# A convolution gate's projection moves from the attention's filler work to a Strassen section of the gate stage

## The chip, the cores and the metric

The kernel runs on one NeuronCore of a Trainium2 chip. The metric is the device time of one execution in microseconds (us), lower is better. TensorE (PE) does the matrix products, VectorE (DVE), ScalarE (ACT) and GpSimd (POOL) the elementwise work, and SyncE (SP), ACT and POOL issue transfers between the memory outside the core (HBM) and the on-chip memory SBUF. Products land in PSUM, which has eight banks of 128 x 512 float32.

## The reference

One layer of a hybrid block, 1024 tokens by 1024 channels, float32. Cut to what matters here:

```python
h = rmsnorm(x, ln1_g) * (1.0 + sc1) + sh1
p = h @ w_in
q, k, v, cb, cc, cx, ga, gb = split(p)          # eight sections of 1024 columns
q, k = rmsnorm(q per head), rmsnorm(k per head) # 16 heads of 64
y_a = stick_breaking_attention(q, k, v)         # strictly causal, 128-query blocks
y_b = cb * causal_dwconv(cc * cx, conv_w)       # conv over three tokens
merged = sigmoid(ga) * (y_a @ w_branch_a) + sigmoid(gb) * (y_b @ w_branch_b)
x = x + g1 * (merged @ w_out)
h = rmsnorm(x, ln2_g) * (1.0 + sc2) + sh2
x = x + g2 * ((silu(h @ w_ffn_gate) * (h @ w_ffn_up)) @ w_ffn_down)
```

In the attention, with z the scaled product of a query and a key, a weight is sigmoid(z) times the product of (1 - sigmoid(z)) over the keys between that key and the query. No softmax is needed, but a running product along the keys is.

## The kernel before, in words

Every float32 product is made of three PE matmuls: each operand is split into a rounded high part and the low rest, and high x high, high x low and low x high are summed in PSUM. The splits are made by one ACT copy and one DVE subtraction, and weights pass through them after they are loaded.

The stages, in order:

- **Start** (to about 205 us): norm statistics, v and k, the factors of h for the next stage, kept in HBM (`d_t`) or in the four large tiles `hh`, `hl`, one pair per half of the tokens.
- **Gate stage** (about 205 to 587 us): five sections of the input projection, in the list `gates`: q (section 5), conv C and conv x (1 and 2, by turns), the two branch gates (4 and 3). A section has four entries, each of two row blocks j and j+4 by two token halves. An entry uses a seven-product form of Strassen (in the Winograd variant): seven half products `half_prod` (lines 131 to 133) of 12 matmuls each in place of eight. POOL forms the sums of weights (`ws`), ACT and DVE split them, DVE combines the products (`c11`, `c12`, `c21`, `c22`), and `put` hands each of the four results on. `later` runs deferred work; for q that is `put_q`, two splits for each result.
- **Attention** (about 587 to 981 us): 16 heads of eight query blocks i, 128 steps s in all. A step computes the scores z of its block (lines 914 and 915), ACT takes the sigmoid (916), POOL masks the diagonal block (919), DVE runs the scan of products over every second key (929) and POOL fills in the other half (137). The transposes of a block (943) come LAG steps later, here two; ACT (946) and DVE (947) split what they give into `ath` and `atl`, and one step after the second block of a pair the product with v follows (958 and 959, tile `o`). So the order in which PE runs them is fixed: PE takes its instructions in the order in which they were written, and so do DVE and POOL for the attention's own.
- Between the attention's instructions stand **fillers**: groups of three matmuls (`mm_ch`, lines 1019 to 1021) of work that needs no attention result. A planner spreads them: each piece of attention work has a cost (`F_Z`, `F_T`, `F_S`), the sum is `ta`, and `fill` emits filler groups, counted as 0.65 each, up to `ta * ratio`. The first HEAD groups run ahead of the first scores, TAIL is kept for the end. The fillers are the conv B projection (section 0) times the convolution's result, 16 tiles of eight groups, and then the product of that with `w_branch_b`, again 16 tiles of eight groups.
- **Later stages**: the product with `w_branch_a`, the output projection, the FFN.

Of the conv branch: `put_u` writes the convolution's result to HBM (`d_y`); the filler loads it (`cy`), multiplies it by its product, splits that and writes it to `d_yb`; the second half of the fillers loads `d_yb` into the four large tiles. Since the gate stage overwrites part of `hh[1]`, `hl[1]` with a factor, that part is first saved to `d_h` and loaded again when the gate stage ends.

SP, ACT and POOL each run their transfers' issues in order. In the built program a transfer issued from SP or ACT also waits for the one eight earlier among those of both.

## Time and profile before

| | |
|---|---|
| times of three runs | 1794.98, 1796.44, 1798.49 us; median 1796.44 |
| profiled execution | 1797.03 us, span 1795.0 us |
| TensorE clock granted, mean | 0.999 |
| busy | PE 1781.7, DVE 1270.1, ACT 829.6, POOL 343.3 us |

A span is the time from the first to the last instruction; the device time holds 2.0 us more. A row "L1019 PE MATMUL pj<-big,whi ... x256 | 113.2, 442" reads: line 1019 of the kernel, engine PE, output tile `pj` from inputs `big` and `whi`, 256 of them, 113.2 us in all, 442 ns each. PE's matmuls are pipelined, so that the length of one says little; what counts is the distance between two starts. A wait in brackets, as in "[2.41 <-POOL pt L137]", is the idle time ahead of an instruction and what ended it.

### The profile page before, as it was taken

Reading aid. Unit: us, or ns where it says so; the run is one execution under the profiler, and the core shown is the slowest. Engines: PE = TensorE matmul, PEld = TensorE weight load, DVE = VectorE, ACT = ScalarE, POOL = GpSimd, SP = SyncE. Lnnn points to the kernel's source line nnn. Section 1 sums busy time; section 2 is a strip of 40 time slices with the busy share of each in tenths; the row PEclk is TensorE's granted clock in tenths of the full one; section 3 lists DMA queues with packets and bytes.
Section 4 is the critical chain, followed back from the end, with each engine's and each line's share of the span. In section 5 each row is a group of like instructions: output and inputs, shape, how many; then the busy total and the mean of one; then the engine's idle time right before and its main releaser. Section 6 shows DMA issues by size and latency. Waiting matters only on the chain.

```text
span 1795.0 us, 24911 instructions
## 1 busy us (share of the span) xinstructions
PE 1781.7 (99%) x8599; PEld 1485.0 (83%) x8599; DVE 1270.1 (71%) x2030; ACT 829.6 (46%) x1553; POOL 343.3 (19%) x437
## 2 busy tenths in 40 slices
PE   8999999999999999999999999999999999999999
PEld 6888877888888788888888888888888888888887
DVE  6876486687774677777776764698877787644776
ACT  5534364333433567776675221764544454432321
POOL 0023333823231244333332100100000000000000
PEclk9999999999999999999999999999999999999999
DMA  9579654222644977796655866334533444389876
GB/s 379 163 240 376 246 192 141 88 87 98 221 152 142 279 209 190 198 326 177 165 139 183 277 223 217 123 106 159 217 129 137 156 174 158 131 331 351 263 233 222
DMA packets 165009, 359.07 MB, mean 200 GB/s; under 512 B 15538, under 2 KB 60938, under 8 KB 163732
## 3 DMA queue, kind: packets, MB, share of 16 engines
q1 hardware_dynamic: 128300, 289.65, 49.3%
q10 hardware_dynamic: 33096, 55.25, 8.7%
q0 software_dynamic: 3488, 12.59, 2.1%
q8 instruction: 68, 1.11, 0.3%
q14 instruction: 57, 0.47, 0.1%
HBM read 247.84 MB, written 109.62 MB: 199 GB/s over the span
## 4 chain that ended last, share of the span: by engine, by line
PE 96%; DMA 2%; ACT 1%; DVE 0%; issue 0%; POOL 0%; SPq 0%; POOLq 0%; DVEq 0%; ACTq 0%
PE e L132 8%; PE e L133 8%; PE e L131 8%; PE pj L131 7%; PE pj L133 7%; PE pj L132 7%; PE pj L294 7%; PE pj L1019 5%; PE pj L1020 5%; PE pj L1021 5%; PE e L1613 4%; PE e L1614 4%; PE e L1615 4%; PE tr L943 3%; PE o L959 2%; PE z L914 2%
## 5 line engine op out<-in xcount | busy, mean ns | idle before, releaser
L1229 ACT ACTIVATE whi<-raw 128x512 fp32r<-128x512 f32 x137 | 84.9, 628 | 159.6 <-PE e L132 101.0
L1230 DVE TENSOR_TENSOR wlo<-raw,whi 128x512 fp32r<-128x512 f32 x137 | 93.1, 687 | 70.2 <-ACT whi L1229 52.8
L137 POOL TENSOR_TENSOR pt<-pt 128x63 f32<-128x63 f32 (+7 forms) x128 | 101.5, 793 | 212.8 <-DVE pt L929 196.5
L132 PE MATMUL e<-big,whi 128*128 128x512 f32 x352 | 136.9, 389 | 0.0
L131 PE MATMUL e<-big,whi 128*128 128x512 f32 x352 | 136.5, 390 | 0.0
L133 PE MATMUL e<-big,wlo 128*128 128x512 f32 x352 | 136.1, 389 | 0.0
L294 PE MATMUL pj<-whi,big 128*128 128x512 f32 x448 | 132.9, 393 | 2.7 <-ACT big L263 2.7
L947 DVE TENSOR_TENSOR atl<-tr,ath 128x512 fp32r<-128x512 f32 (+1 forms) x192 | 104.0, 553 | 34.0 <-ACT ath L946 32.7
L137 DVE TENSOR_TENSOR c<-pj,c 128x512 f32<-128x512 f32 x140 | 93.4, 683 | 47.6 <-PE pj L133 47.0
L131 PE MATMUL pj<-big,whi 128*128 128x512 f32 x320 | 125.0, 391 | 0.0
L133 PE MATMUL pj<-big,wlo 128*128 128x512 f32 x320 | 124.8, 390 | 0.0
L132 PE MATMUL pj<-big,whi 128*128 128x512 f32 x320 | 124.6, 389 | 0.0
L1614 PE MATMUL e<-wlo,f 128*128 128x512 f32 (+1 forms) x319 | 121.8, 382 | 0.0
L1613 PE MATMUL e<-whi,f 128*128 128x512 f32 (+1 forms) x319 | 121.6, 382 | 0.0
L1615 PE MATMUL e<-whi,f 128*128 128x512 f32 (+1 forms) x319 | 121.6, 382 | 0.0
L916 ACT ACTIVATE pt<-z,rq 128x128 f32<-128x128 f32 (+1 forms) x192 | 107.3, 579 | 25.7 <-PE z L915 23.0
L1019 PE MATMUL pj<-big,whi 128*128 128x512 f32 x256 | 113.2, 442 | 0.0
L137 DVE TENSOR_TENSOR wlo<-raw,whi 128x512 fp32r<-128x512 f32 x108 | 86.2, 802 | 30.6 <-ACT whi L517 30.4
L946 ACT ACTIVATE ath<-tr 128x512 fp32r<-128x512 f32 (+1 forms) x192 | 93.1, 488 | 28.6 <-PE tr L943 27.6
L131 PE MATMUL e<-rh,whi 128*128 128x512 f32 x264 | 102.7, 389 | 0.0
L132 PE MATMUL e<-rl,whi 128*128 128x512 f32 x264 | 102.7, 389 | 0.0
L294 PEld LDWEIGHTS pj<-whi,big 128*128 128x128 f32 x448 | 84.4, 189 | 21.8 <-ACT big L263 4.2
(301 smaller groups left out, 4736.9 us busy)
## 6 DMA issues: line engine op xcount, KB each, us to landing
f<-d_f SPq DMA_DIRECT2D x77, 512.0 KB, 4.5
d_f<-fs SPq DMA_DIRECT2D x70, 512.0 KB, 3.4
raw<-w_cg SPq DMA_DIRECT2D x40, 512.0 KB, 3.7
raw<-w_u SPq DMA_DIRECT2D x26, 512.0 KB, 4.2
raw<-w_g SPq DMA_DIRECT2D x25, 512.0 KB, 4.3
raw<-w_kv SPq DMA_DIRECT2D x20, 512.0 KB, 5.0
ld<-ada SPq DMA_DIRECT2D x16, 512.0 KB, 7.0
d_t<-ts SPq DMA_DIRECT2D x16, 512.0 KB, 6.7
```

The lines of the kernel that those rows point to most:

```text
L131: nc.tensor.matmul(ps, wh[:, k, :], fh[:, k, :], start=(k == 0 and not onto), stop=False, skip_group_check=onto)
L132: nc.tensor.matmul(ps, wh[:, k, :], fl[:, k, :], start=False, stop=False, skip_group_check=onto)
L133: last = nc.tensor.matmul(ps, wl[:, k, :], fh[:, k, :], start=False, stop=(k == 3), skip_group_check=onto)
L137: eng.tensor_tensor(out=out, in0=a, in1=b, op=op)
L294: nc.tensor.matmul(ps, a, b, start=(k == 0 and q == 0), stop=(k == KT - 1 and q == 2))
L916: nc.scalar.activation(pt[:, off + s0:off + s0 + m], z[:, :m], AF.Sigmoid, scale=rq[:, 1, i, h:h + 1])
L946: nc.scalar.activation(th[:, :nb, c0:c0 + P], src, AF.Copy)
L947: nc.vector.tensor_tensor(out=tl[:, :nb, c0:c0 + P], in0=src, in1=th[:, :nb, c0:c0 + P].bitcast(F32), op=ALU.subtract)
L1019: nc.tensor.matmul(ps, wh, rh_, start=(k == 0), stop=False)
L1613: nc.tensor.matmul(o, sh, w[0][:, c], start=(j == 0), stop=False)
L1614: nc.tensor.matmul(o, sh, w[1][:, c], start=False, stop=False)
L1615: nc.tensor.matmul(o, sl, w[0][:, c], start=False, stop=(j == NJ - 1))
```

## The change

Conv B is taken out of the fillers and becomes a further section (0) of the gate stage's list, behind conv C and x and ahead of the branch gates. `load_y` loads the convolution's result for an entry's two row blocks, and `put_b`, called from `later`, multiplies, splits and writes to `d_yb`, on the ACT queue. The save and reload of `d_h` go. The four large tiles are allocated in another order, so that the fillers' first pair, `yh[0]`, `yl[0]`, takes the place of `hh[0]`, `hl[0]`; the second pair is loaded later.

The attention's transposes come three steps behind the scores (LAG), the product with v four steps behind (DAV), with six tiles `pt` in place of five. The first head's q, k and v are loaded from the POOL queue, and the second head's loads no longer wait in the planned order for the first head's. HEAD falls from 16 to 4, the fillers' total is halved, and up to 5.0 units (EARLY) of it are moved to the attention's first steps.

```diff
-    hh = [big() for n in range(2)]
-    hl = [big() for n in range(2)]
+    hh, hl = [], []
+    for n in range(2):
+        hh.append(big())
+        hl.append(big())
...
-             [(sec, j) for sec in (4, 3) for j in range(4)])
+             [(sec, j) for sec in (0, 4, 3) for j in range(4)])
...
+    def load_y(m):
+        ys[m] = g_big()[:, :T]
+        nc.sync.dma_start(ys[m], d_y[m])
+
+    def put_b(c, m, n):
+
+        hl_ = gp.tile([P, 2, 512], F32R, tag=("sq", "tr")[n], bufs=2, name=nm("gt"))
+        tt(nc.vector, c, c, ys[m][:, n * 512:(n + 1) * 512], ALU.mult)
+        nc.scalar.activation(hl_[:, 0], c, AF.Copy)
+        tt(nc.vector, hl_[:, 1], c, hl_[:, 0].bitcast(F32), ALU.subtract)
+        for e in range(2):
+            nc.scalar.dma_start(d_yb[e][n][:, m, :], hl_[:, e].bitcast(F32))
...
+        if sec == 0:
+            load_y(j)
+            load_y(j + 4)
...
+            elif sec == 0:
+                pendb.append((c, m, n))
...
+            if pendb:
+                put_b(*pendb.pop(0))
...
-    NPT = 5
+    NPT, LAG = 6, 3
...
-    NZ, NTR, NPJ, DAV, KQ = 2, 3, 2, 3, 1
+    NZ, NTR, NPJ, DAV, KQ = 2, 3, 2, LAG + 1, 1
...
-                    with tc.issue_after(lastld[0].ins):
+                    with tc.issue_after(lastld[0].ins) if h else ExitStack():
                         att_load(h + 1)
...
-            tr_ = att_trans(*steps[s - 2]) if 0 <= s - 2 < len(steps) else iter(())
+            tr_ = att_trans(*steps[s - LAG]) if 0 <= s - LAG < len(steps) else iter(())
...
-        cb_w = {}
-        for m, n in [(m + d, n) for m in range(0, KT, 2) for n in range(2) for d in range(2)]:
...
-                mm_ch(ps, w, hh[n], hl[n], kk, kk + KQ)
-            nc.vector.tensor_tensor(out=y, in0=ps, in1=y, op=ALU.mult)
...
+        load_yb(0)
         wb = {}
...
+            if (m, n) == (1, 0):
+                with tc.issue_after(lastld[0].ins):
+                    load_yb(1)
...
-    FILL = 2.0 * 16 * 5.2
+    FILL = 16 * 5.2
-    HEAD, TAIL = 16, 10.0
+    HEAD, TAIL, EARLY = 4, 10.0, 5.0
-    ratio = (FILL - TAIL) / ATT
+    ratio = (FILL - TAIL - EARLY) / ATT
...
-        att_load(0)
+        att_load(0, nc.gpsimd)
+        vl = load_vlast(0, nc.gpsimd)
+        turn_vlast(0, vl)
+        load_v(0, 1, nc.gpsimd)
+        load_v(0, 0, nc.gpsimd)
...
-            fill(min(ta * ratio, FILL - TAIL) + 1.3 * nfl)
+            fill(min(ta * ratio + min(1.5 * ta, EARLY), FILL - TAIL) + 1.3 * nfl)
```

The rows that follow are the built programs' instruction order, engine by engine; line numbers are each kernel's own. PE's order around the first transposes, from the transposes of `vl` (v's last rows) on; `pj` is a filler, `z` the scores, `tr` transposes. Before:

```order
L871 MATMUL tr_5149<-dm,vl_5115 64x9 x8
L1019 MATMUL pj_5243<-big_144,whi_5130 128x512
L1020 MATMUL pj_5243<-big_146,whi_5130 128x512
L1021 MATMUL pj_5243<-big_144,wlo_5131 128x512
L914 MATMUL z_5250<-skh_5120,sqt_5119 128x256
L915 MATMUL z_5250<-skl_5121,sqt_5119 128x256
L914 MATMUL z_5262<-skh_5120,sqt_5119 128x384
L915 MATMUL z_5262<-skl_5121,sqt_5119 128x384
L1019 MATMUL pj_5243<-big_144,whi_5130 128x512
L1020 MATMUL pj_5243<-big_146,whi_5130 128x512
L1021 MATMUL pj_5243<-big_144,wlo_5131 128x512
L943 MATMUL tr_5272<-dm,pt_5110 128x128
```

After:

```order
L890 MATMUL tr_5808<-dm,vl_5793 64x9 x8
L933 MATMUL z_5890<-skh_5798,sqt_5797 128x384
L934 MATMUL z_5890<-skl_5799,sqt_5797 128x384
L1038 MATMUL pj_5846<-big_5826,whi_5838 128x512
L1039 MATMUL pj_5846<-big_5827,whi_5838 128x512
L1040 MATMUL pj_5846<-big_5826,wlo_5839 128x512
L933 MATMUL z_5915<-skh_5798,sqt_5797 128x512
L934 MATMUL z_5915<-skl_5799,sqt_5797 128x512
L1038 MATMUL pj_5942<-big_5826,whi_5924 128x512
L1039 MATMUL pj_5942<-big_5827,whi_5924 128x512
L1040 MATMUL pj_5942<-big_5826,wlo_5925 128x512
L962 MATMUL tr_5946<-dm,pt_5787 128x128
```

Ahead of these rows stand, before, only the first block's scores; after, those, two filler groups, the second block's scores and one more group. So five filler groups and three further blocks' scores now lie between the first scores and their transposes, where there were two groups and two blocks.

PE's order where the first head ends, from the second transposes of block 5 on, with the product with v of blocks 4 and 5 (`o`); in both kernels four transposes of block 5 and one filler group stand just ahead. Before:

```order
L943 MATMUL tr_5456<-dm,pt_5110 128x128 x2
L914 MATMUL z_5472<-skh_5279,sqt_5278 128x128
L915 MATMUL z_5472<-skl_5280,sqt_5278 128x128
L1019 MATMUL pj_5442<-big_144,whi_5196 128x512
L1020 MATMUL pj_5442<-big_146,whi_5196 128x512
L1021 MATMUL pj_5442<-big_144,wlo_5197 128x512
L943 MATMUL tr_5484<-dm,pt_5111 128x128 x4
L1019 MATMUL pj_5442<-big_144,whi_5196 128x512
L1020 MATMUL pj_5442<-big_146,whi_5196 128x512
L1021 MATMUL pj_5442<-big_144,wlo_5197 128x512
L958 MATMUL o_5494<-ath_5385,vt_5259 128x256
L959 MATMUL o_5494<-atl_5386,vt_5259 128x256
```

After:

```order
L962 MATMUL tr_6125<-dm,pt_5786 128x128 x2
L933 MATMUL z_6132<-skh_5906,sqt_5905 128x256
L934 MATMUL z_6132<-skl_5907,sqt_5905 128x256
L962 MATMUL tr_6141<-dm,pt_5787 128x128 x4
L977 MATMUL o_6148<-ath_6058,vt_5887 128x256
L978 MATMUL o_6148<-atl_6059,vt_5887 128x256
```

Both filler groups between the transposes and the product that uses them are gone here.

SP's order when the attention begins: the loads of the second filler pair and of the second head (`sqt`, `skh`, `skl`). Before, from the reload of `d_h` on:

```order
L1099 DMA big_146<-d_h_88 128x2048
L1099 DMA big_144<-d_h_87 128x2048
L834 DMA sqt_5119<-d_q_63 64x1024
L835 DMA skh_5120<-d_k_65 64x8x128
L836 DMA skl_5121<-d_k_66 64x8x128
```

After, the end of the second pair's eight loads and the start of the second head's:

```order
L1055 DMA big_5932<-d_yb_70 128x1024
L1056 DMA big_5933<-d_yb_72 128x1024
L505 DMA raw_7536<-w_b 128x1024
L1045 DMA sgi_5822<-d_sgb 128x512
L853 DMA sqt_5905<-d_q_63 64x1024
L854 DMA skh_5906<-d_k_65 64x8x128
L855 DMA skl_5907<-d_k_66 64x8x128
```

Before, SP loads 2 MB of `d_h` and then the first head; after, it loads 8 MB of `d_yb` in two pairs, the second of which waits for the gate stage's last product, and then the second head.

More of the change, by code (lines that the diff above doesn't have):

```diff
@@ L81, in block_kernel @@
     d_t = {q: drp.tile([P, 2, 4, 512], F32, name=f"d_t{q}") for q in (6, 3, 5, 4)}
-    d_h = [drp.tile([P, 4, 512], F32, name=f"d_h{e}") for e in range(2)]
     ident = const.tile([P, P], F32, name="dm")
@@ L833, in att_load, with load_v @@
             es = slice(e * DH, (e + 1) * DH)
-            nc.sync.dma_start(sqt[es].bitcast(F32), d_q[e][pr, e0:e0 + DH, :])
-            nc.sync.dma_start(skh[es].rearrange("p (i t) -> p i t", t=P).bitcast(F32), d_k[0][pr // 4][:, e0:e0 + DH, pr % 4].rearrange("i p t -> p i t"))
-            nc.sync.dma_start(skl[es].rearrange("p (i t) -> p i t", t=P).bitcast(F32), d_k[1][pr // 4][:, e0:e0 + DH, pr % 4].rearrange("i p t -> p i t"))
+            q.dma_start(sqt[es].bitcast(F32), d_q[e][pr, e0:e0 + DH, :])
+            q.dma_start(skh[es].rearrange("p (i t) -> p i t", t=P).bitcast(F32), d_k[0][pr // 4][:, e0:e0 + DH, pr % 4].rearrange("i p t -> p i t"))
+            q.dma_start(skl[es].rearrange("p (i t) -> p i t", t=P).bitcast(F32), d_k[1][pr // 4][:, e0:e0 + DH, pr % 4].rearrange("i p t -> p i t"))
         hd[h] = (sqt, skh, skl)
-    def load_v(h, e):
+    def load_v(h, e, q=nc.sync):
         pr = h // 2
@@ L844, in load_v @@
         vab[t_] = first_va if (h, e) == (0, 1) else v_tile(e)
-        lastld[0] = nc.sync.dma_start(vab[t_], d[e:P + e])
+        lastld[0] = q.dma_start(vab[t_], d[e:P + e])
     def att_dv(h, part):
@@ L1023, in fillers @@
     def fillers():
-        cb_w = {}
-        for m, n in [(m + d, n) for m in range(0, KT, 2) for n in range(2) for d in range(2)]:
-            if n == 0:
-                with tc.issue_after(lastld[0].ins) if m > 1 else ExitStack():
-                    cb_w[m] = load_ch(w_cg[0, m])
-            w = cb_w[m]
-            y = fp.tile([P, 512], F32, tag="st", bufs=3, name=nm("cy"))
-            nc.sync.dma_start(y, d_y[m, :, n * 512:(n + 1) * 512])
-            ps = ps_f()
-            for kk in range(0, KT, KQ):
-                if kk:
-                    yield 0.65 * KQ
-                mm_ch(ps, w, hh[n], hl[n], kk, kk + KQ)
-            nc.vector.tensor_tensor(out=y, in0=ps, in1=y, op=ALU.mult)
-            yh = fq.tile([P, 512], F32R, tag="ybh", bufs=2, name=nm("ybh"))
-            yl = fq.tile([P, 512], F32R, tag="ybl", bufs=2, name=nm("ybl"))
-            nc.scalar.activation(yh, y, AF.Copy)
-            nc.vector.tensor_tensor(out=yl, in0=y, in1=yh.bitcast(F32), op=ALU.subtract)
-            nc.sync.dma_start(d_yb[0][n][:, m, :], yh.bitcast(F32))
-            nc.sync.dma_start(d_yb[1][n][:, m, :], yl.bitcast(F32))
-            yield 0.65 * KQ
         def load_sb(m, n):
@@ L1051, in fillers, with load_yb @@
         yh, yl = [], []
-        for n in range(2):
+        def load_yb(n):
             yh.append(big())
```

20 lines of the change are left out of this document (5 added, 15 removed).

## The prediction

> **What bounds the kernel now.** I read the page first: busy times, slices, and the chain that ended last.
>
> ```profile
> span 1795.0 us, 24911 instructions
> PE 1781.7 (99%) x8599; PEld 1485.0 (83%) x8599; DVE 1270.1 (71%) x2030; ACT 829.6 (46%) x1553; POOL 343.3 (19%) x437
> PEclk9999999999999999999999999999999999999999
> PE 96%; DMA 2%; ACT 1%; DVE 0%; issue 0%; POOL 0%; SPq 0%; POOLq 0%; DVEq 0%; ACTq 0%
> ```
>
> PE is busy 99% of the span at the full clock and is 96% of the chain. So a change pays by PE time that it removes, less any wait that it opens on PE. The view by stretches shows which engines could open one:
>
> ```profile
> 205.00:281.00 76.00, 76.00 (x335) 59.90 (x334) 60.53 (x89) 45.76 (x79) 24.17 (x16) 1.00 0.56 196
> 434.00:587.00 153.00, 153.00 (x678) 126.63 (x677) 105.27 (x153) 58.68 (x98) 40.83 (x29) 1.00 0.50 170
> 587.00:598.00 11.00, 11.00 (x50) 9.13 (x49) 1.98 (x3) 2.37 (x4) 0.00 (x0) 1.00 0.86 259
> 598.00:981.00 383.00, 379.07 (x2340) 329.43 (x2339) 294.56 (x504) 264.12 (x588) 144.31 (x260) 1.00 0.74 206
> ```
>
> The columns are the length, then busy time of PE, PEld, DVE, ACT and POOL, clock, DMA share, GB/s. The rows are the q section, the branch-gate sections, the 16 filler groups ahead of the first scores, and the attention. PE has no idle time in the first three and 3.9 us in the attention, nearly all at its start.
>
> **The PE work.** Distances between starts on PE's timeline:
>
> ```profile
> 584.73 0.39 PE L131 MATMUL pj<-big,whi 128*128 128x512 f32 x1
> ...
> 587.45 0.39 PE L1019 MATMUL pj<-big,whi 128*128 128x512 f32 x1
> ...
> 598.33 0.22 PE L914 MATMUL z<-skh,sqt 128*128 128x128 f32 x1
> ...
> 707.48 0.60 PE L943 MATMUL tr<-dm,pt 128*128 128x128 f32 x4
> 707.84 0.48 PE L1019 MATMUL pj<-big,whi 128*128 128x512 f32 x1
> 708.15 0.40 PE L1020 MATMUL pj<-big,whi 128*128 128x512 f32 x1
> 708.39 0.39 PE L1021 MATMUL pj<-big,wlo 128*128 128x512 f32 x1
> 708.62 0.38 PE L943 MATMUL tr<-dm,pt 128*128 128x128 f32 x2
> 708.76 0.30 PE L914 MATMUL z<-skh,sqt 128*128 128x128 f32 x1
> 708.90 0.28 PE L915 MATMUL z<-skl,sqt 128*128 128x128 f32 x1
> 709.01 0.44 PE L1019 MATMUL pj<-big,whi 128*128 128x512 f32 x1
> ...
> 709.76 0.60 PE L943 MATMUL tr<-dm,pt 128*128 128x128 f32 x4
> 710.11 0.48 PE L1019 MATMUL pj<-big,whi 128*128 128x512 f32 x1
> ...
> 710.89 0.28 PE L958 MATMUL o<-ath,vt 128*128 128x256 f32 x1
> ```
>
> A half product of 12 takes 587.45 - 584.73 = 2.72 us, 0.2267 each. In the attention a filler matmul takes about 0.235 (708.15 to 708.39 to 708.62), and 0.31 (707.84 to 708.15) behind transposes.
>
> Removed: conv B as filler, 16 tiles x 8 x 3 = 384 matmuls. By the two instruction orders 336 of them leave the stretch between the first scores and the last product with v (705 fillers there become 369): 336 x 0.235 = 79.0 us. The extra 0.08 behind transposes does not leave with a filler, since something else then follows; but the places where another instruction follows transposes fall from 194 to 171, 23 x 0.08 = 1.8. The other 48 stood ahead of the scores (16 groups become 4) or behind the attention: 48 x 0.2267 = 10.9. Together -91.7 us.
>
> Added: four gate entries of 7 x 12 matmuls, 336 x 0.2267 = 76.2 us, if none waits. Its cover: `put_b` has per result two DVE operations, one ACT copy and two ACT issues, while `put_q` has two DVE operations, three ACT ones and two issues; and the q section above runs PE without a gap at DVE 60.5 of 76. The loads of y on SP stand behind weight loads; DVE has the sums in hand for the next entry, half an entry ahead, so I take 0 (no gain is possible there, since these matmuls have no shorter form). If that cover fails and each of four entries waits for a load of 7 us (rows below), it is 28 us. SP is rid of the fillers' 16 loads of y and 32 writes of `d_yb` in the attention; the writes move to ACT, as many as q has there.
>
> Net PE work: 76.2 - 91.7 = -15.5 us. All the rest is about waits.
>
> **The start of the attention.** Its wait now:
>
> ```profile
> 601.37 0.40 PE L915 MATMUL z<-skl,sqt 128*128 128x512 f32 x1
> 604.17 0.44 PE L943 MATMUL tr<-dm,pt 128*128 128x128 f32 x2 [2.41 <-POOL pt L137]
> 602.61 0.69 DVE L137 TENSOR_TENSOR vb<-vb,va 128x512 f32<-128x512 f32 x1 [2.85 <-DMA vb<-d_v]
> 593.85 0.43 SPq L845 DMA_DIRECT2D vb<-d_v  x1
> PE tr L943 <- POOL pt L137: 2.8, 2, 2.4
> PE o L958 <- ACT ath L946: 0.9, 1, 0.9
> ```
>
> DVE stood at `vb`, which landed 8.7 us after its issue, with the second block's scan queued behind it, and PE lost 2.8 us. After the change POOL issues this load, but only behind `vl`, which must wait until the seventh product of the last entry has read the tile below it, 2.7 us ahead of the gate stage's end. That is some 586.5 on the old clock, 7 us earlier than now, so landing near 595; POOL has ten such issues and nothing behind them until the first mask; the second transposes come, by the order and the distances above, 10 us behind the gate's last product, at 597.4. So this wait goes, -2.8.
>
> What is late next are the second head's loads. On SP they stand behind the second `d_yb` pair, 4 MB that cannot start before 587.45, when its tiles are free.
>
> ```profile
> 580.00:585.00 5.00, 5.00 (x24) 4.14 (x23) 2.80 (x6) 1.15 (x2) 0.00 (x0) 1.00 1.03 362
> 760.00:770.00 10.00, 10.00 (x65) 8.82 (x64) 6.45 (x14) 6.92 (x16) 3.34 (x8) 1.00 1.06 389
> big<-d_yb SPq DMA_DIRECT2D x16, 512.0 KB, 7.1
> skl<-d_k SPq DMA_DIRECT2D x32, 256.0 KB, 7.0
> ```
>
> At a full DMA share the core moves 362 to 389 GB/s. From 587.45 on, 4 MB of `d_yb`, 1 MB of v and 0.75 MB of weights and gates need 15 to 16 us, to about 603; the last of the second head's loads, issued when the end of that lands, take 7.0 more at worst and 3 at best: 606 to 610. Those scores are due, by order and distances, 18.7 us after the gate's end, at 606.2. So the wait is between 0 and about 4; with the v loads' share of the same engines as little sure as it is, I allow 6. I take 2.8, so that the start is even: 0 (range -2.8 to +3.2). The second filler pair itself is read right behind those scores and lands before them.
>
> The Trainium skill, page "DMA: Bandwidth & Descriptors", section "Issuing engines are not separate DMA queues", speaks against the POOL issues: transfers from all three queues run on the same 16 engines, so another queue saves only issue time. By that rule the first head's loads gain what they gain from standing free of SP's order, and the sum would have 2.8 us more, 1790.3; the DMA share of 1.03 above agrees with shared engines.
>
> **Less cover in the attention.** Between a block's transposes and the product with v, ACT splits and DVE subtracts. Two cases:
>
> ```profile
> 704.31 0.60 ACT L946 ACTIVATE ath<-tr 128x512 fp32r<-128x512 f32 x1 [0.38 <-PE tr L943]
> 705.62 0.68 DVE L947 TENSOR_TENSOR atl<-tr,ath 128x512 fp32r<-128x512 f32 x1
> 710.45 0.60 ACT L946 ACTIVATE ath<-tr 128x512 fp32r<-128x512 f32 x1 [0.77 <-PE tr L943]
> 711.08 0.69 DVE L947 TENSOR_TENSOR atl<-tr,ath 128x512 fp32r<-128x512 f32 x1
> 703.67 0.60 PE L943 MATMUL tr<-dm,pt 128*128 128x128 f32 x4
> ```
>
> From the transposes' end at 710.11 to 711.77 is 1.66 us with DVE free; from 704.03 (703.67 and 0.36) to 706.30 is 2.27 with a filler's multiplication ahead on DVE. Against that stand, from 707.84 to 710.89, 3.05 us of other PE work, so no wait. In the new order two filler groups are gone from that place: 0.78 + 0.14 + 0.33 + 0.35 = 1.60, and 0.12 more until `atl` is read. I worked this through all 64 products with v: with a need of 1.62 us the shortfalls sum to 1.1 us, at 2.0 to 6.6 (35 products), at 2.2 to 13.6, at 2.4 to 21, at 2.6 to 31; in the old order 0.2 at 2.0. I take 2.0, the middle of the two cases: **+6.6 us**.
>
> The other chain, scores to transposes, gets a third step: where the old order leaves 4.3 to 7.0 us by block (the middle of the 16 heads), the new leaves 5.2 to 8.3. It costs nothing unless DVE falls behind, and by the stretch above DVE would have 294.6 - 16 x (0.69 + 0.69 + 0.87) = 259 busy in about 302 us, 85% where it has 77%:
>
> ```profile
> L1041 DVE TENSOR_TENSOR ybl<-cy,ybh 128x512 fp32r<-128x512 f32 x16 | 11.1, 691 | 0.8 <-ACT ybh L1040 0.7
> L1037 DVE TENSOR_TENSOR cy<-pj,cy 128x512 f32<-128x512 f32 x15 | 10.3, 688 | 7.4 <-PE pj L1021 6.5 <-DMA cy<-d_y 0.6
> L137 DVE TENSOR_TENSOR wlo<-raw,whi 128x512 fp32r<-128x512 f32 x30 | 26.0, 870 | 3.4 <-ACT whi L517 3.3
> ```
>
> Sum: -15.5 + 0 + 6.6 = -8.9 us on the profiled 1797.03: 1788.1. The median stands 0.59 lower, so **1787.5**.
>
> **Rivals.** (1) The full gain: the splits keep near 1.66 and all loads are in time: -15.5 - 2.8 + 1.1 = -17.2, so 1779.2. For it: before, PE waited only 0.9 us for these products. Against: the cover halves. (2) Late loads: `d_yb` and the second head run 6 to 8 us late and the filler weights with them: 1787.5 + 5 = 1792.5, up to 1796. For it: the DMA shares over 1.0; against: the page's 7.0 us is a median under such load. The page "TensorE: Matmul & The Clock Gate", Part 1, of the Trainium skill adds that PE idle for a window of about 3.4 us falls to half its clock until it has been busy as long; by that figure such a wait would cost some 1.7 us more. The 2.4 us wait above left the clock at 1.00, and no longer one is in the attention. (3) Slower: DVE at 85% puts the subtraction behind a scan or a weight split each time, the need goes to 2.6 and the products wait 31 us: 1787.5 - 6.6 + 31 = 1812. It decides from a need of about 2.25 us on, where the shortfalls eat the 15.5. For it: 2.27 occurs in the trace; against: one multiplication of a filler stood there, and half of those are gone. (4) The change does not do what it says: the counts in the order rule that out for PE; for the first head's loads it would show as an unchanged wait, +2.8, 1790.3.
>
> **Chances.** Forecast 0.48 (0.46 of it faster by over 0.2%, 3.6 us, which is what a measurement can tell from no change), full gain 0.18, late loads 0.14 (0.06 faster, 0.07 same, 0.01 slower), slower 0.12 (0.03 same, 0.09 slower), the unchanged first loads and anything else 0.08 (0.03 faster, 0.03 same, 0.02 slower). Together 0.73 faster, 0.15 same, 0.12 slower. The forecast's own range is 1783 to 1792. The whole range goes from the full gain, 1778, to a need of 2.4 us, 1787.5 - 6.6 + 21 = 1802.
>
> **What would show it.** Right: 24 gate entries in about 457 us without PE gaps; fillers in the attention halved; the attention 302 to 312 us from the first scores to the last product with v; new PE waits at `o` for ACT or DVE of some 7 us; no wait at `tr` near the start, a wait of up to 6 us at the first scores of the second head. Wrong: PE gaps in section 0, waits at `tr` for POOL all through the attention, or waits at `o` of over 15 us.

## The result: slower by 40 us

| | before | after |
|---|---|---|
| median, and all runs | 1796.45 us (1794.98 to 1798.49, 4 runs) | 1836.62 us (1836.2 to 1838.4, 4 runs) |
| ratio, 95% interval | | 1.0225 (1.0207 to 1.0242) |
| profiled execution, span | 1797.03, 1795.0 us | 1836.86, 1835.1 us |
| first scores start at | 598.3 us | 667.4 us |
| from there to the start of the last product with v | 382.3 us | 347.2 us |
| from there to the end of the span | 814.4 us | 820.5 us |

The forecast was 1787.5 us with a range to 1802; the time lies 49 us above the forecast and outside the range. The head of the page after, its chain of waits and the view by stretches (columns as in the prediction):

```profile
PE 1791.5 (98%) x8551; PEld 1483.2 (81%) x8551; DVE 1298.4 (71%) x2070; ACT 827.8 (45%) x1569; POOL 370.3 (20%) x463
...
PE 82%; DVE 5%; DMA 5%; issue 3%; ACT 2%; POOL 2%; SPq 0%; POOLq 0%; ACTq 0%; DVEq 0%
```

```profile
434.00:663.00 229.00, 229.00 (x1012) 189.59 (x1012) 164.67 (x242) 86.38 (x146) 70.89 (x52) 1.00 0.61 206
663.00:667.00 4.00, 4.00 (x20) 3.30 (x19) 2.44 (x4) 2.32 (x4) 0.55 (x2) 1.00 1.07 387
667.00:1015.00 348.00, 320.88 (x2012) 273.76 (x2011) 261.90 (x457) 232.41 (x554) 141.22 (x262) 0.98 0.64 167
1015.00:1835.00 820.00, 810.35 (x3618) 670.24 (x3616) 562.85 (x907) 321.19 (x557) 17.97 (x38) 0.99 0.57 200
```

PE was 96% of the chain and is 82%; DVE, DMA and ACT have entered it. The gate stage runs without a gap (229.00 of 229), as forecast. The attention does not: PE is idle for 27 of 348 us, where it was for 4 of 383. What PE waited for from the gate stage's end to 1100 us, by line (columns: waited for, us in total, times, longest):

```profile
PE z L933 <- ACT pt L935: 13.2, 7, 7.9
PE o L978 <- DVE atl L966: 6.1, 15, 1.5
PE pj L1038 <- DVE sgi L1193: 4.7, 3, 4.1
PE o L977 <- DVE oy L984: 3.8, 6, 1.2
PE o L977 <- ACT ath L965: 1.3, 2, 1.0
PE tr L962 <- DVE atl L966: 1.0, 1, 1.0
```

Three things are seen: one long wait at the scores, many short ones at the products with v, and one behind the attention. By stretches, in us:

| | forecast | measured | miss |
|---|---|---|---|
| up to the first scores (76.2 - 36 x 0.2267) | +68.0 | +69.1 | 1 |
| attention (-80.8 and +6.6) | -74.2 | -35.1 | 39 |
| behind it (12 matmuls fewer) | -2.7 | +6.1 | 9 |

**The start.** POOL's, DVE's and PE's timelines there, and two stretches:

```profile
662.43 0.61 POOL L881 DMA_DIRECT2D vl<-d_v  x1 [18.58 <-PE pj L132]
...
668.82 0.57 POOL L864 DMA_DIRECT2D va<-d_v  x1 [5.27 <-ACT pt L935]
```

```profile
678.91 0.69 DVE L136 TENSOR_TENSOR vb<-vb,va 128x512 f32<-128x512 f32 x1 [8.35 <-DMA vb<-d_v]
...
687.48 0.69 DVE L1073 TENSOR_TENSOR mb<-pj,sgi 128x512 f32<-128x512 f32 x1 [6.37 <-DMA sgi<-d_sgb]
```

```profile
672.70 0.27 PE L962 MATMUL tr<-dm,pt 128*128 128x128 f32 x1
680.89 0.48 PE L933 MATMUL z<-skh,sqt 128*128 128x128 f32 x1 [7.92 <-ACT pt L935]
...
682.34 0.63 PE L1040 MATMUL pj<-big,wlo 128*128 128x512 f32 x1
682.76 0.63 PE L933 MATMUL z<-skh,sqt 128*128 128x512 f32 x1
```

```profile
664.00:681.00 17.00, 9.08 (x49) 7.14 (x47) 3.50 (x8) 4.00 (x9) 2.44 (x7) 0.86 1.01 393
681.00:700.00 19.00, 16.17 (x71) 13.40 (x72) 10.04 (x18) 8.85 (x22) 5.69 (x11) 0.76 0.98 261
```

The issue of `va` waits 5.3 us behind that of `vl`. In the built program it waits for a write to `d_sga` of the last gate entry, whose tile it overwrites (head16's row below names it; "ACT pt" here is merely what happened last). `vb` is issued right behind, at 669.4, and lands 9.4 us later, beside a DMA share of 1.01. DVE stands at `vb`, ACT at the copy behind it, that copy stands ahead of the sigmoids on ACT, the sigmoids free the banks of the scores, and PE waits 7.9 us. Then DVE stands again, at a gate load `sgi` that SP issued behind 8 MB of `d_yb`, and PE loses 2.8 us more. After each wait the clock is at half: the distance of two matmuls is 0.42 (682.34 to 682.76) in place of 0.23. PE worked some 9 us at that clock, so it cost some 4 us.

### The profile page after: what moved, and what is told of

Same layout as the page of the kernel before. It is cut to its first block, busy times and chain, and to the rows that moved or that the text cites. A ratio compares the mean times of both kernels' runs of the same rounds, so it can differ in the third digit from the quotient of the medians.

```text
span 1835.1 us, 24912 instructions
## 1 busy us (share of the span) xinstructions
PE 1791.5 (98%) x8551; PEld 1483.2 (81%) x8551; DVE 1298.4 (71%) x2070; ACT 827.8 (45%) x1569; POOL 370.3 (20%) x463
## 4 chain that ended last, share of the span: by engine, by line
PE 82%; DVE 5%; DMA 5%; issue 3%; ACT 2%; POOL 2%; SPq 0%; POOLq 0%; ACTq 0%; DVEq 0%
PE e L131 8%; PE e L132 8%; PE e L130 8%; PE pj L132 8%; PE pj L130 8%; PE pj L131 8%; PE pj L295 7%; PE e L1615 4%; PE e L1616 4%; PE e L1614 4%; PE pj L1038 2%; PE tr L962 2%; PE pj L1040 2%; PE pj L1039 2%; PE o L978 2%
## 5 line engine op out<-in xcount | busy, mean ns | idle before, releaser
L1230 ACT ACTIVATE whi<-raw 128x512 fp32r<-128x512 f32 x137 | 84.9, 628 | 159.7 <-PE e L131 103.5
L136 DVE TENSOR_TENSOR c<-pj,c 128x512 f32<-128x512 f32 x168 | 112.2, 683 | 62.6 <-PE pj L132 61.7
L130 PE MATMUL pj<-big,whi 128*128 128x512 f32 x384 | 149.9, 390 | 0.0
L132 PE MATMUL pj<-big,wlo 128*128 128x512 f32 x384 | 149.7, 390 | 0.0
L131 PE MATMUL pj<-big,whi 128*128 128x512 f32 x384 | 149.5, 389 | 0.0
L1231 DVE TENSOR_TENSOR wlo<-raw,whi 128x512 fp32r<-128x512 f32 x137 | 92.9, 686 | 66.5 <-ACT whi L1230 49.0
L948 DVE TENSOR_TENSOR_SCAN pt<-pt 128x64 f32<-128x64 f32 (+7 forms) x128 | 96.4, 753 | 24.2 <-POOL pt L938 23.8
L130 PE MATMUL pj<-ft,whi 128*128 128x512 f32 x288 | 112.2, 390 | 0.3 <-ACT whi L516 0.3
L131 PE MATMUL pj<-ft,whi 128*128 128x512 f32 x288 | 112.1, 389 | 0.0
L132 PE MATMUL pj<-ft,wlo 128*128 128x512 f32 x288 | 111.7, 389 | 0.0
L516 ACT ACTIVATE whi<-raw 128x512 fp32r<-128x512 f32 x104 | 64.9, 628 | 96.9 <-PE pj L131 64.1
L516 ACT ACTIVATE whi<-ws 128x512 fp32r<-128x512 f32 x96 | 58.5, 627 | 108.2 <-PE pj L131 46.9
```

The lines of the kernel that those rows point to most:

```text
L130: nc.tensor.matmul(ps, wh[:, k, :], fh[:, k, :], start=(k == 0 and not onto), stop=False, skip_group_check=onto)
L131: nc.tensor.matmul(ps, wh[:, k, :], fl[:, k, :], start=False, stop=False, skip_group_check=onto)
L132: last = nc.tensor.matmul(ps, wl[:, k, :], fh[:, k, :], start=False, stop=(k == 3), skip_group_check=onto)
L136: eng.tensor_tensor(out=out, in0=a, in1=b, op=op)
L516: nc.scalar.activation(hi, src, AF.Copy)
L948: nc.vector.tensor_tensor_scan(out=both, data0=first, data1=both, initial=1.0, op0=ALU.mult, op1=ALU.mult)
```

## Is the attention bound by PE at all?

**nofill** takes all fillers out of the attention and runs them behind it.

```diff
-            fill(min(ta * ratio + min(1.5 * ta, EARLY), FILL - TAIL) + 1.3 * nfl)
+            fill(0)
```

> The change with no filler inside the attention: 4 groups ahead, 124 behind it. Shows the attention's own pace. PE's work there is 347.2 - 39.9 - 369 x 0.235 = 220.6 us, DVE's about 260. Theory 'PE bounds': 225 to 250 us from the first scores to the last product with v, total 1815 to 1835. Theory 'a floor of the chains, near the time that PE needs with half the fillers': 285 to 325 us, total 1870 to 1900.

Measured: 1892.57 us in one run; the attention takes 323.6 us with no filler. With 369 filler matmuls it takes 347.2 and with 705 (before) 382.3. Three kernels' middle of the attention, nofill first, then after, then before:

```profile
700.00:960.00 260.00, 220.44 (x1365) 180.91 (x1364) 203.62 (x357) 186.77 (x459) 113.61 (x217) 0.95 0.59 139
```

```profile
700.00:1000.00 300.00, 283.63 (x1823) 242.83 (x1823) 243.09 (x425) 215.72 (x517) 130.93 (x241) 1.00 0.59 147
```

```profile
620.00:960.00 340.00, 339.83 (x2118) 296.84 (x2117) 267.08 (x458) 239.19 (x538) 131.64 (x239) 1.00 0.72 198
```

This is the finding on which the rest hangs. The attention has a floor of its own: nofill's 323.6 less the two long waits at its own start (7.9 and 1.5 us on PE's timeline) is some 314 us. That is an upper bound, since nofill also has the lower clock (0.95 in the row, 0.91 over the whole attention, where the change has 0.98): PE worked some 46 us of it at half clock, which cost up to 23, so the floor at full clock lies between some 291 and 314. It was measured for the new order alone. Before, PE's work (382) lay some 70 to 90 us above that, and the rounds through ACT, POOL and DVE were hidden. With half the fillers PE's work without waits is about as long as the floor: the mean distances of before by kind, without its own waits (z 0.194, transposes 0.082, fillers 0.250, products 0.118), times the counts of after (407, 592, 369, 639) give 295 us. Two things that take nearly as long, in fixed orders that wait for each other, take longer than either: 347.2, or some 332 without the two waits of the start (11 us) and the half clock behind them (some 4). So the first half of the fillers is cheap (369 matmuls for 23.6 us, 0.064 each; with the half clock taken out of both runs at most 0.11), and the half that was moved out was worth 35 us there, or some 50 without the loss at the start, not 81. In the gate stage it costs 76.

**head128** was meant to show the same with the fillers ahead of the scores: `HEAD` from 4 to 128.

> The change with all 128 filler groups ahead of the first scores, so that the attention has none: its own pace is seen. PE's own work there is 347.2 - 39.9 (lost) - 369 x 0.235 = 220.6 us; DVE's is some 80% of 347 less the fillers' 16 + 16 operations of 0.69, some 256 us. Theory 'PE bounds the attention and waits are exceptions': 225 to 245 us from the first scores to the last product with v, total 1815 to 1830. Theory 'the chains over ACT, DVE and POOL set a floor that half the fillers no longer hide': 290 to 330 us there, total 1870 to 1910.

Measured: 1887.94 us, ratio 1.051 (1.0495 to 1.0526). It does not answer the question, since the order ahead of the scores is the scheduler's: 315 of the filler matmuls (105 groups) stayed in the attention, at other places, and it took 371.7 us. Where the fillers stand seems to matter as much as how many there are; that was not tried by itself.

## What sets the floor: the round through the other engines

One of the recurring waits, on DVE's and on PE's timeline:

```profile
758.76 1.23 DVE L948 TENSOR_TENSOR_SCAN pt<-pt 128x512 f32<-128x512 f32 x1 [0.59 <-POOL pt L938]
760.01 0.43 DVE L984 TENSOR_TENSOR oy<-o,otmp 64x256 f32<-64x256 f32 x1
760.47 1.02 DVE L966 TENSOR_TENSOR atl<-tr,ath 128x512 fp32r<-128x512 f32 x2
```

```profile
758.80 0.60 PE L962 MATMUL tr<-dm,pt 128*128 128x128 f32 x4
760.59 0.35 PE L977 MATMUL o<-ath,vt 128*128 128x256 f32 x1 [1.18 <-DVE oy L984]
761.22 0.38 PE L978 MATMUL o<-atl,vt 128*128 128x256 f32 x1 [0.28 <-DVE atl L966]
```

DVE first stands 0.59 us for POOL's mask, then scans 1.23 us, and only then adds `oy`, which frees the one bank `o`; the subtraction `atl` is behind that. PE needs both. Five runs test this round.

**scanlast** puts the scan behind the addition.

```diff
             yield from tr_
+            yield from av_
             if s < len(steps):
                 att_scan(*steps[s])
-            yield from av_
```

> The change with the scan of a step put behind the addition that frees the bank of the product with v (on DVE the two change places; the order on PE stays). Theory 'the one bank o': the addition stands behind a scan that itself waits for POOL's mask, so the next product waits (3.8 us for oy, and part of the 6.1 for atl behind it): 4 to 9 us less than the change, 1828 to 1833. Rival 'DVE is simply behind': what the products gain the transposes lose by later scans, 1835 to 1840.

Measured: 1832.42 us, ratio 1.02 (1.0181 to 1.022), some 4 us less than the change, at the edge of what the two intervals tell apart. The waits for `oy` are gone, those for `atl` have grown from 6.1 to 13.0 us in the same stretch:

```profile
PE o L978 <- DVE atl L966: 13.0, 17, 1.4
```

The total lies just within what "the one bank o" expected, the rows agree with the rival: most of the wait moved within the round.

**lag2** gives the transposes back their two steps, the product with v its three and `pt` its five tiles.

```diff
-    NPT, LAG = 6, 3
+    NPT, LAG = 5, 2
```

> The change with the transposes two steps behind the scores and five buffers, as before; conv B stays in the gate stage. Theory 'the third step is needed with half the fillers': the chain of sigmoid, mask, scan and multiplication has some 1.5 us less per block, transposes wait for POOL 1 to 2 us per head, 15 to 35 us slower than the change: 1852 to 1872. Rival 'the third step itself costs': the waits at the products with v in the new order come from the third step, 1815 to 1826.

Measured: 1829.91 us, ratio 1.0182 (1.0167 to 1.0197), 6.7 us less than the change. Neither theory: the waits at the products fall and those at the transposes return.

```profile
PE tr L962 <- POOL pt L136: 8.5, 17, 1.1
PE z L933 <- ACT pt L935: 3.5, 8, 0.6
PE o L978 <- DVE atl L966: 2.7, 6, 0.6
```

Listed waits are 15 us here and 15 in the change between 700 and 1000 us, and the attention is 2.8 us shorter, with 12 filler matmuls fewer in it (357). The third step moves the waits from one end of the round to the other and gains nothing.

**scanshort** cuts every scan to its last 64 pairs.

```diff
-        first = pt[:, slice(D - 1, off, -2)]
-        both = pt[:, slice(D - 2, off - 1 if off else None, -2)]
+        first = pt[:, slice(D - 1, D - P, -2)]
+        both = pt[:, slice(D - 2, D - P - 1, -2)]
```

> The change with each scan cut to its last 64 pairs, so that DVE has 128 x (0.753 - 0.29) = 59 us less work in the attention (leaves out: the running product over the rest of each row; every instruction and its order stay). Theory 'DVE, in order and 80% busy, sets the floor': the waits behind the start fall from 25 us to under 10, 13 to 18 us less than the change, 1818 to 1824. Rival 'the floor is the latency of the round ACT, POOL, DVE or ACT's own work': 0 to 5 us less, 1831 to 1837.

Measured: 1814.57 us, ratio 1.0098 (1.0083 to 1.0114), 22 us less than the change and more than the theory expected; the attention takes 328.2. From 700 us on the waits at the products are nearly gone (11.7 us in the change):

```profile
PE o L978 <- DVE atl L966: 0.7, 2, 0.4
```

**nomask** takes POOL's mask out; DVE's work stays.

```diff
-            if s0 + m == n:
-                diag = pt[:, D - P:]
-                nc.gpsimd.affine_select(out=diag, in_=diag, ...)
```

> The change without POOL's mask on the last 128 columns of each block (leaves out: the mask over the diagonal; 128 POOL instructions of 0.29 us and the wait of DVE's scan for them, 23.8 us in 46 places). Theory 'a scan that waits at the head of DVE's queue holds the addition and the subtraction behind it, and PE with them': the waits behind the start fall from 25 to 10 to 17 us, 8 to 15 us less than the change, 1822 to 1829. Rival 'only DVE's work counts': 0 to 4 us less, 1832 to 1837.

Measured: 1820.98 us, ratio 1.0136 (1.0122 to 1.015), 15.6 us less; the attention takes 335.7. The rival, that only DVE's amount of work counts, falls: DVE does the same work and the waits at `o` shrink from 11.7 to 4.6 us.

**vpool** takes 22 us of work from DVE and gives it to POOL.

```diff
-            tt(nc.vector, dv, dv, va[:, :, cs], ALU.subtract)
+            tt(nc.gpsimd, dv, dv, va[:, :, cs], ALU.subtract)
...
-        tt(nc.vector, vt[:, :, DH:], dv, vt[:, :, :DH].bitcast(F32), ALU.subtract)
+        tt(nc.gpsimd, vt[:, :, DH:], dv, vt[:, :, :DH].bitcast(F32), ALU.subtract)
```

> The change with the two DVE operations per head on v (vb less va, and the low part of vt; 32 x 0.68 = 22 us) on POOL. A relief of DVE that keeps the result. Theory 'DVE's work sets the floor': scanshort gave 22 us for 59 us of DVE work, so 22 x 22 / 59 = 8 us less than the change, 1826 to 1831. Rival 'POOL stands in the round too': its mask and multiplication wait behind these 32 operations of some 1.3 us, and the scans with them: 1835 to 1845.

Measured: 1855.32 us, ratio 1.0319 (1.0303 to 1.0336), 19 us more than the change, the rival's direction and more than it expected; in the profiled execution, 1849.81 us, the attention takes 363.1. DVE's stretch and its waits for the mask, vpool first, then the change:

```profile
700.00:1000.00 300.00, 274.21 (x1734) 231.10 (x1734) 215.55 (x380) 206.30 (x496) 145.37 (x262) 0.99 0.58 143
```

```profile
DVE pt L948 <- POOL pt L938: 46.0, 49, 2.0
```

```profile
DVE pt L948 <- POOL pt L938: 18.9, 43, 0.7
```

DVE is busy 72% of the time (215.55 of 300) where it was 81% (243.09), and the kernel is slower. POOL's added work did not slow DVE's own operations: a scan took 746 ns on average, in the change 757. So DVE's load alone does not set the floor. What fits all these runs is the length of the round PE, ACT, POOL, DVE, POOL, PE with each engine's work in one fixed order: a shorter scan or no mask shortens it, a longer POOL queue stretches it.

## What the start costs

**sp1** undoes one part: the first head's loads go back to SP.

```diff
-        att_load(0, nc.gpsimd)
-        vl = load_vlast(0, nc.gpsimd)
+        att_load(0)
+        vl = load_vlast(0)
         turn_vlast(0, vl)
-        load_v(0, 1, nc.gpsimd)
-        load_v(0, 0, nc.gpsimd)
+        load_v(0, 1)
+        load_v(0, 0)
```

> The change with the first head's ten loads issued by SP, as before. In SP's order the second d_yb pair then falls behind v and sgi, since the tie that holds it behind the last load of v acts on one queue only. The step of the prediction (POOL's issues save the wait of 2.8 us): slower than the change by 3 to 8 us, 1839 to 1845. Theory 'flood': the pair behind v is worth more than the queue, so 4 to 10 us less than the change, 1826 to 1833, though the first head's loads now stand behind 4 MB of the first pair and the first scores may wait up to 5 us.

Measured: 1836.67 us, ratio 1.0211 (1.0194 to 1.0227): the same as the change, and between what the two theories expected. The attention is 9.4 us shorter and starts 11.0 us later, since now the first scores wait:

```profile
PE z L933 <- DMA skh<-d_k: 12.2, 1, 12.2
```

**b_pool** is that part alone, on the kernel before: `att_load(0)`, `load_vlast(0)` and both `load_v` are given `nc.gpsimd`.

> The kernel before with one part of the change alone: the first head's ten loads issued by POOL. The step of the prediction: the wait of 2.8 us at the first transposes goes, 1793.6. Theory now: va waits for the last write of the gate stage and for the DMA engines, not for SP, so the wait stays or grows: 1796 to 1800.

Measured: 1802.08 us, ratio 1.0029 (1.0019 to 1.0039), 5 us slower than before and above both expectations. The first head's v did come earlier: `vb` landed at 599.5, where in the kernel before DVE stood for it until 602.6. But another load was late in its place: DVE now stood at a filler's load of y, issued by SP, and behind it PE at the scores, with half clock after that (the distance of two matmuls 0.43, 603.87 to 604.30):

```profile
DVE cy L1037 <- DMA cy<-d_y: 6.3, 1, 6.3
```

```profile
602.64 0.69 PE L914 MATMUL z<-skh,sqt 128*128 128x384 f32 x1 [3.52 <-ACT pt L916]
```

So this part gains nothing on either kernel.

**head16** and **yblate** shift the work or the loads; **yb16** does both.

```diff
-    HEAD, TAIL, EARLY = 4, 10.0, 5.0
+    HEAD, TAIL, EARLY = 16, 10.0, 5.0
```

> The change with 16 filler groups ahead of the first scores in place of 4; nothing else. Theory 'v late': the loads of the first head's v land at a time that the DMA engines set (va issued 668.8, 5.3 us behind vl, since it waits for the last gate entry's tile to be written out), some 11.5 us behind the first scores, so PE work put ahead of the scores eats the two waits of 7.9 and 3.0 us and the half clock behind them (some 5 us): 10 to 16 us less than the change, 1821 to 1827 us, and a start without a wait of over 2 us. Rival 'the start is owed to the DMA rate': d_yb, v and the second head's loads share the engines at a share of 1.0, so a wait of the same size turns up at the next scores, 1832 to 1837. Second rival 'cover': twelve groups fewer inside the attention open 8 us of other waits, 1829 to 1835.

Measured: 1842.57 us, ratio 1.0252 (1.0236 to 1.0267), 6 us slower than the change. All three theories miss. With 16 groups, two tiles, done, the next group needs a bank whose eviction waits for the gate `sgi`, and that load is late:

```profile
DVE mb L1073 <- DMA sgi<-d_sgb: 29.3, 2, 23.7
...
PE pj L1038 <- DVE mb L1073: 14.7, 1, 14.7
...
POOL va L864 <- DMA d_sga<-c: 5.2, 1, 5.2
```

The edit of yblate, where `lastsp` is the last SP load of `sgi` or of a head, and `load_yb(1)` moves from the start of tile (1, 0) to its fifth group:

```diff
-            if (m, n) == (1, 0):
-                with tc.issue_after(lastld[0].ins):
-                    load_yb(1)
...
+                if (m, n, kk) == (1, 0, 4):
+                    with tc.issue_after(lastsp[0].ins):
+                        load_yb(1)
```

> The change with the second d_yb pair (8 loads, 4 MB) behind the second head's loads and the first two loads of the gates sgi in SP's order, where it stood ahead of them; the order on PE is the same. Theory 'flood': from 664 to 680 the DMA engines run at a share of 1.0 and 374 to 419 GB/s, and that pair is what fills them; it holds back v (lands 678.9, 11.5 us behind the first scores) and sgi (lands 687, 6.4 us of waiting on DVE with the scan and the second block's vb behind it). Then the waits of 8.1 and 3.0 us and the half clock behind them shrink: 8 to 14 us less than the change, 1822 to 1829 us, and the 25 us of small waits later in the attention stay. Rival 'the write that va waits for sets it': va's issue comes at 668.8 whatever the loads do, and lands 4 us later at best, 673: the wait shrinks by 5, no more, 1830 to 1832. Second rival: the pair is late for its own fillers, nothing gained, 1834 to 1840.

Measured: 1833.66 us, ratio 1.0194 (1.0179 to 1.021), 3 us less, which the two intervals do not tell apart. The gate is in time and the wait of 2.8 us gone; v lands no earlier (679.6, in the change 678.8):

```profile
PE tr L963 <- POOL pt L136: 7.7, 1, 7.7
```

> The change with the second d_yb pair behind the second head's loads (as in the run yblate) and 16 filler groups ahead of the first scores in place of 4. In yblate the gates sgi land at 671 and the first head's v at 679.7, and PE stands 7.7 us at the second block's transposes with some 4 us of half clock behind. Theory 'v lands at its own time': 12 groups, 12 x 3 x 0.2267 = 8.2 us, put ahead of the scores now eat that wait, with no gate late as in the run head16: 10 to 13 us less than yblate, 1820 to 1824 us. Rival 'cover': the 12 groups are missing inside the attention and open as much there, 1830 to 1835.

Measured: 1840.3 us, ratio 1.024 (1.0226 to 1.0254), above both expectations. The 17th group is the first that reads the second pair, which is now late for it:

```profile
PE pj L1039 <- DMA big<-d_yb: 10.0, 1, 10.0
```

Whatever is put first, something else lands late. So the last pair of runs took the bytes away. **noyb** lets the fillers multiply with `hh` and `hl`, which are there:

```diff
-        load_yb(0)
+        yh, yl = hh, hl
         wb = {}
...
-            if (m, n) == (1, 0):
-                with tc.issue_after(lastld[0].ins):
-                    load_yb(1)
```

> The change without the 16 loads of d_yb, 8 MB: the fillers multiply the weights with hh and hl, which stand in SBUF as they did for conv B in the kernel before (leaves out: conv B's result in the product of branch B). The order on PE stays. Theory 'flood': these 8 MB arrive just between the gate stage and the attention, where the kernel before had fillers that needed no load, and they are what makes v, sgi and the write ahead of v late: the first 40 us lose under 5 us in place of 15, 10 to 15 us less than the change, 1822 to 1827 us; the 25 us of small waits behind stay. Rival 'v is late by its own chain' (vl behind the seventh product, then the write of the last entry, then 4 to 5 us of landing): the wait of 8.1 shrinks to 4 to 6, 1829 to 1833.

Measured: 1826.71 us, ratio 1.0167 (1.0151 to 1.0182), 9.9 us less than the change; the attention takes 338.4. One wait is left at the start:

```profile
PE z L933 <- ACT pt L935: 7.3, 6, 4.9
```

Both theories hold in part. The 8 MB cost 10 us: 3 us of the first wait, the second wait and part of the half clock; v's own chain, `vl` behind a product of the last entry and `va` behind a write of it, leaves a wait of 4.9 us without them. It is not v's landing that the 8 MB made slow: `va` is issued at 666.6, 2.2 us earlier than in the change, but `vb` still takes 8.9 us to land, against 9.4.

**noyb_scan** takes both causes away at once: the edits of noyb and of scanshort together.

> Both: no loads of d_yb, and each scan cut to its last 64 pairs (leaves out what the runs noyb and scanshort leave out). Theory 'two causes that add up': the gain of scanshort over the change, 22 us, and that of noyb, 10 to 15, together 32 to 37: 1800 to 1805 us, with under 12 us lost on PE in the attention. Rival 'one floor': with the start gone the rest is bound by DVE again and they do not add: 1808 to 1814.

Measured: 1807.04 us, ratio 1.0055 (1.0038 to 1.0072), 29.6 us less than the change, of 32.0 for the two apart (22.05 and 9.9). The time lies between the two expectations, nearer to the first, and PE is idle for 10.1 us in the attention, as that one had it (under 12): the two nearly add, so there are two causes, not one. What is left of the miss is about 20 us: v's wait of 5.4 us with its half clock, some 8 us behind the attention, and short waits.

## The kernel before, once more

**b_head20** gives before four more groups ahead of the scores: `HEAD` from 16 to 20.

> The kernel before with 20 filler groups ahead of the first scores in place of 16. With all fillers the attention has 382 us of PE work against a floor of some 306 (run nofill, 323.6 less 17.7 at its start), so four groups can leave without opening a wait, and 4 x 3 x 0.2267 = 2.7 us of work ahead of the scores eat the wait of 2.8 at the first transposes: 1793.4 to 1795. Rival 'the wait follows the scores': unchanged, 1796 to 1798.

Measured: 1802.03 us, ratio 1.0025 (1.0014 to 1.0035), slower by 5, which neither theory expected. Here too the scheduler had its way: the groups ran behind the first scores (597.66), and the wait stayed. Its size did not change, but what followed it did. Before first, as the prediction showed it: a wait of 2.41 us, then matmuls at 0.23 from 604.68 on. Then b_head20, and its clock in the stretch behind the wait beside that of before:

```profile
604.68 0.39 PE L1020 MATMUL pj<-big,whi 128*128 128x512 f32 x1
604.91 0.39 PE L1021 MATMUL pj<-big,wlo 128*128 128x512 f32 x1
```

```profile
605.77 0.79 PE L914 MATMUL z<-skh,sqt 128*128 128x512 f32 x1 [2.39 <-ACT pt L916]
...
608.35 0.63 PE L1020 MATMUL pj<-big,whi 128*128 128x512 f32 x1
608.78 0.63 PE L1021 MATMUL pj<-big,wlo 128*128 128x512 f32 x1
```

```profile
605.00:612.00 7.00, 5.78 (x17) 4.29 (x18) 4.18 (x9) 4.44 (x10) 3.27 (x7) 0.54 0.95 305
```

```profile
605.00:612.00 7.00, 6.56 (x37) 5.33 (x36) 5.68 (x11) 4.65 (x11) 3.71 (x6) 1.00 1.07 347
```

In these 7 us, of which the last 0.8 of the wait and one more of 0.45 are part, PE ran 17 matmuls in place of 37. No run here beats the kernel before.

## Why the prediction was wrong, step by step

- **The PE work** (-91.7 and +76.2) was right where PE is the bound: the first scores start 69.1 us later, forecast 68.0, and the gate section has no gap at DVE 164.67 of 229.
- **"336 x 0.235 = 79.0 us" in the attention** is the step that failed. It prices a filler by PE's time, which holds as long as PE is the bound. The prediction read from the stretches that it was (379 of 383) and asked which waits would open, but not how long the attention takes without fillers. nofill answers 323.6 us with its start, so of 382 only some 70 to 90 us were above the floor, and the 302 to 312 us that the prediction named as right lay about at it. Measured: -35.1 in place of -74.2; of these 39 us some 15 were lost at the start (below), the other 24 here, and scanshort and nomask give back 22 and 16 us by shortening the round.
- **"Less cover", +6.6 us**, had the right place and the wrong rule. It counted one need (2.0 us from transposes to `atl`) against PE's work in between. The waits listed at `o` are 11.7 us. The one bank `o` and the scan ahead of `oy` were not in it. Nor do listed waits hold all that is lost: a matmul is counted busy for 0.39 us where the next could start after 0.23, so that part of each short wait counts as busy. Of 52 us that the attention takes beyond the 295 of its work, PE's idle time shows 27.
- **"The z to tr chain costs nothing" with the third step** was right on its rows (one wait of 1.0 us at `tr`), but no gain: lag2 shows the waits only change ends.
- **The start, "even"**, failed in "only behind `vl`": `va` also waited for the last entry's write, 5.3 us. In b_pool, on the old clock, `vb` landed at 599.5, where the prediction had 595. And the sum of bytes asked only when the second head's loads would land, not when v and `sgi` would. The prediction noted that the second `d_yb` pair stood ahead on SP; it did not see why. In the source it is tied behind the last load of v, and in sp1, with that load on SP, the pair stands behind it; with the load on POOL the pair runs ahead. Moving ten issues to another queue moved 4 MB on the first one (so sp1 changes both at once). The page "DMA: Bandwidth & Descriptors" of the Trainium skill, section "Issuing engines are not separate DMA queues", had spoken against the POOL issues, and sp1 and b_pool agree with it: those issues are worth nothing in the change and cost 5 us in the kernel before.
- **Behind the attention** nothing was forecast but -2.7. The product with `w_branch_a` now reaches its gates before they land, where the kernel before has no wait at all behind the attention, and the clock halves again for some 5 us (row below). Fewer filler matmuls are left over ahead of it, 3 in place of 15, but that this is the cause is not shown: lag2 has 15 left, as before, and still waits 2.4 us there.

```profile
1049.94 0.77 PE L1038 MATMUL pj<-ya,whi 128*128 128x512 f32 x1 [4.05 <-DVE sgi L1193]
```

- **The rivals.** "Slower", 1812, had the sign and the kind (a subtraction behind a scan), but gave it to DVE's load of 85%; it was 81%, and vpool shows that load is not what decides. It was priced 24.5 us above the forecast, and the attention without its start missed by some 24; that is luck, since the waits at `o` that it priced at 31 us are 11.7. "Late loads", 1792 to 1796, had the other half, priced at 5 to 8.5 us where the start lost some 15. No case had both together.

That the small waits come from this round was shown by taking scan and mask away. Why the three-step order costs 6.7 us against lag2 was not settled (5.8 between the profiled executions, of which 2.8 in the attention and 2.5 behind it).

## What to carry to other kernels

Taking a filler out saves its own time only as long as the engine that runs it, and not the round through the other engines, sets the length of the stage; so before taking fillers out, ask for the floor: how long the stage takes with none. Where the engine's work and that floor come close, as 295 and some 291 to 314 us here, the stage took longer than either (some 332). And when a load changes its queue, look at what was ordered by it on the old one.

## What was not expected of the hardware

- Two waits of the same length, 2.41 and 2.39 us, left the clock at 1.00 in the kernel before and at one half in b_head20, from 605.6 to 612.4. The page "TensorE: Matmul & The Clock Gate", Part 1, of the Trainium skill says the window of some 3.4 us runs freely, so that the phase matters; that agrees: the stretches of half clock are one, two or three times 3.4 us long (in the change 690.0 to 693.4 and 676.3 to 686.6), and b_head20's begins just when its wait ends. The page also gives a whole idle window for the drop; here less idle time was enough. So a wait's price can be some 3 us above its length (half of the 6.2 us that PE worked at half clock in b_head20), or not.
- Short waits alone do it too. In nofill no wait of PE from 700 us on is longer than 2.3 us, and the clock was at one half in ten stretches there. One of them, with the 3.2 us ahead of it, in which PE was busy for 1.53:

```profile
709.10:712.30 3.20, 1.53 (x10) 1.09 (x10) 2.57 (x4) 1.64 (x4) 1.79 (x4) 1.00 1.10 222
712.40:715.80 3.40, 3.40 (x17) 3.30 (x17) 1.30 (x5) 1.11 (x3) 0.54 (x2) 0.50 0.90 154
```

- In the change a DMA share of 1.0 lasted some 30 us at the end of the gate stage, at 332 to 419 GB/s by stretches of 10 us. In it a load of 512 KB (`vb`) took 9.4 us from issue to landing; but it took 8.9 in noyb too, without the 8 MB and at 286 GB/s (666.6 to 676.0, share 0.95). The seven later loads of `vb` in the change have a median of 3.4.
